# A decoder block on one core: VectorE and ScalarE issue in the order of emission from step 12 to step 172

## The chip, the cores and the metric

The kernel runs on one core of one Trainium2 chip. The metric is the device time of one execution in microseconds (us), the lower the better. The engines are named as the profile names them: PE is TensorE's matmul, PEld its weight load, DVE is VectorE, ACT is ScalarE, POOL is GpSimd, SP is SyncE, which only issues DMAs here. A queue of an engine is told by a q behind its name.

## The reference: what is computed

One decoder layer on 256 tokens of 2048 channels, all in float32. A normalized input goes through one wide projection. Its columns feed two mixers that run beside each other:

- an S5 branch: a state-space scan over the 256 positions (64 groups, 64 complex states each), then GELU, a gated linear unit (GLU) and a projection;
- an attention branch (DSA): a small indexer scores the keys, the 64 best keys of a query stay, then softmax attention on 8 heads, and a projection.

```python
(u, z_ssm, c_q, k, v, z_attn, k_idx, w_idx, gate_ssm, gate_attn) = jnp.split(proj, pts, axis=-1)
y_ssm = s5_branch(u, ...) * jax.nn.silu(z_ssm)
y_attn = dsa_branch(q, k, v, q_idx, k_idx, w_idx) * jax.nn.silu(z_attn)
merged = jax.nn.sigmoid(gate_ssm) * (y_ssm @ w_ssm_out) + jax.nn.sigmoid(gate_attn) * (y_attn @ w_attn_out)
x = x + merged @ w_o
x = x + jax.nn.sigmoid(rms_norm(x, g_ple) @ w_ple_gate) * rms_norm(p @ w_ple, g_ple_post)
return rms_norm(x, g_final)
```

## The kernel before, in words

**Weights in units.** All weights come from HBM in 254 units of up to 128 x 1024 values (tile `raw`, five buffers, 512 KB each, issued by SP on L99). Each unit is split in two parts for the matmul: ACT rounds it to `hi` (`unit_hi`, L261), DVE subtracts it to get the rest, `lo` (`unit_lo`, L273). `hi` and `lo` have four buffers each. PE multiplies each unit in three passes (weights hi, weights lo, and the low part of the input).

**Steps.** One step works on one unit. Step `s` emits, in this order: what the unit needs; the matmuls of unit `s`; `unit_hi(s + 3)` on ACT; the evacuations that are due (`run_deferred`: DVE or ACT reads the PSUM tile of a block that ended a step earlier); `unit_lo(s + 2)` on DVE; the DMA of unit `s + 7` on SP; and then `pump(BUDGET)`. So `lo` is emitted two steps before PE needs it. The units in order: 0 to 15 the S5 input, 16 to 31 its SiLU gate, 32 to 63 one merge gate, 64 to 79 the attention's SiLU gate, 80 to 103 three quarters of the other merge gate, 104 to 131 the query, key, value and indexer projections, 132 to 147 the GLU, 148 to 155 the rest of that gate, 156 to 171 the S5 branch's projection, from 172 on the attention's projection and all that follows. A unit of the gates has 12 matmuls of 512 columns, one of most other projections 24 of 256 columns.

**Threads.** Work that is no weight unit runs in Python generators, which `pump` advances a little in each step: each piece that a generator emits has a cost (`yield 1.15`), `pump` gives out 1.3 a step (at most 3.0 saved up), and `yield ("lag", n)` puts a generator to sleep for n steps. Such threads are the tables of the S5 branch (`s5_tables`, L834 and below), its scan (`s5_gen` with `cmadd`, L950 to L957: 76 DVE operations for each half of the states, two halves), its output (`s5_out`), and the attention (`attn_gen`: scores, the top-k by `max` and `match_replace`, softmax, output of 8 heads). Where a unit needs the end of a thread, the rest of it is emitted at once (`drain`): that is so before step 104, 132 and 172, the last for the attention.

**Order on an engine.** The program is not issued as emitted. A scheduler walks through it on a model of the engines and gives each engine a fixed sequence: of the instructions that its model finds ready, the one emitted first goes first; one that is not ready in the model is passed by later ones. On the chip each engine then follows its sequence, and semaphores hold an instruction until its inputs are there. So DVE's sequence may hold pieces of a thread ahead of a `lo` that was emitted many steps earlier.

The loop that emits the steps is the end of the function below (L1225 and on).

Of the kernel before, what the change touches and what calls it, by code (L numbers as in the profile page):

```python
# [29 lines left out]
NC = 4  # L30
CW = 512
OFF = 16
NWARM = 30
BUDGET = 1.3
TRLAG = 2
# [9 lines left out]
def block_kernel(ctx: ExitStack, tc: tile.TileContext, A: dict, out: bass.AP):  # L45
# [18 lines left out]
    def slot(tag, shape, dt=F32):  # L64
        return cp.tile(shape, dt, tag=tag, name=nm(tag))

    def const(s, shape, dt=F32):
        return cp.tile(shape, dt, tag=s, name=s)
# [19 lines left out]
    def issue_unit(between=None):  # L88
        n = dma_next[0]
        if n >= len(units):  # L90
            return
        c, h, cols = units[n][:3]
        kind, idx = chunks[c]
        r = wp.tile([P, 1024], F32, tag="raw", name=nm("raw"), bufs=5)
        src = (A["wts"][idx] if kind == "w" else A["wvk"][idx])[:, h * cols:(h + 1) * cols]
        q = 2 if between else 1
        for i in range(q):
            s = slice(i * cols // q, (i + 1) * cols // q)
            nc.sync.dma_start(r[:, s], src[:, s])  # L99
            if between and i == 0:  # L100
                between()
        raws[n] = r
        dma_next[0] += 1
# [36 lines left out]
    def mm(o, l, r, start=True, stop=True, **kw):  # L140
        PE.matmul(o, l, r, start=start, stop=stop, **kw)  # L141
# [51 lines left out]
    def run_deferred(flush=False):  # L193
        while True:
            due = [d for d in deferred if flush or d[0] <= step[0]]
            if not due:
                return
            for d in due:
                deferred.remove(d)
            for d in due:  # L200
                d[1]()
# [26 lines left out]
    def pump(budget):  # L228
        credit[0] = min(credit[0] + budget, 3.0)
        while credit[0] > 0:  # L230
            ready = [t for t in threads if t[1] <= step[0]]
            if not ready:
                return
            credit[0] -= advance(ready[0])

    def drain(t):
        while not t[2]:
            advance(t)
# [13 lines left out]
    def unit_hi(u):  # L252
        if u >= len(units):
            return
        cols = units[u][2]
        hi = unit_tile("hi", u)
        src = raws[u][:, :cols]
        q = 2 if u < 3 else 1
        for i in range(q):
            o = slice(i * cols // q, (i + 1) * cols // q)  # L260
            S.copy(hi[:, o], src[:, o])  # L261
        his[u] = hi

    def unit_lo(u):
        if u >= len(units):
            return
        cols = units[u][2]
        lo = unit_tile("lo", u)
        src = raws.pop(u)
        q = 2 if u < 3 else 1  # L270
        for i in range(q):
            o = slice(i * cols // q, (i + 1) * cols // q)
            TT(lo[:, o], src[:, o], his[u][:, o].bitcast(F32), ALU.subtract)  # L273
        los[u] = lo
# [94 lines left out]
    def big_slot(tag, off=0):  # L369
        t = slot(tag, [P, KT * T + OFF], F32R)  # L370
        return t[:, off:off + KT * T].rearrange("p (k t) -> p k t", t=T)
# [254 lines left out]
    def ev_o(nb):  # L626
# [9 lines left out]
        def f(h, ps):  # L636
            if nb == 0 and h == 0:
                R["x2"] = slot("S1", [P, 2, D])
                R["x2h"] = big_slot("XH", OFF)
                R["x2l"] = big_slot("XL", OFF)  # L640
                R["sq2"] = const("sq2", [P, 2, NC])
# [373 lines left out]
    def attn_gen():  # L1015
# [63 lines left out]
        yield ("lag", 1)  # L1079
        ya = big_slot("S7", OFF).rearrange("p (c h) t -> p c h t", c=2)  # L1080
        R["ya"] = ya
# [128 lines left out]
    S.activation(first, mhalf, AF.Copy)  # L1210
    for i in range(NWARM):
        mm(wps[:, :T], warm[:, :P], warm)
# [9 lines left out]
    for i in range(2):  # L1222
        issue_unit()
    NU = len(units)
    for s in range(NU):  # L1225
        step[0] = s
        fn, need = units[s][3:]
        for n in need or ():
            if callable(n):
                n()  # L1230
            else:
                run_deferred()
                drain(R[n])
        fn(his.pop(s), los.pop(s))
        unit_hi(s + 3)
        run_deferred()
        unit_lo(s + 2)
        issue_unit()
        pump(BUDGET)
# [120 lines left out]
```

## Time and profile before

| | us |
|---|---|
| median of three runs | 788.1 |
| the three runs | 788.07, 788.1, 790.91 |
| the profiled execution, its own time | 790.16 |
| its span, from the first to the last instruction | 788.3 |
| PE busy | 766.6 (97%) |
| PEld busy | 668.2 (85%) |
| DVE busy | 576.5 (73%) |
| ACT busy | 392.1 (50%) |
| granted TensorE clock, mean | 0.997 |

The profiled execution is 2.06 us above the median and near the slowest of the three. Matmuls overlap: one of 512 columns shows as 0.39 us busy, while the next starts 0.23 us after it. So a row of PE that follows a wait costs the wait and also the overlap that is lost. The profile puts a wait down to the line whose result came last.

### The profile page before, as it was taken

What the parts mean: (1) busy time and instruction counts of PE and PEld (TensorE: products, weight loads), DVE (VectorE), ACT (ScalarE), POOL (GpSimd) and SP (SyncE); (2) the same over time, 40 slices, a digit from 0 to 9 for tenths busy, and PEclk for the clock granted to TensorE, in tenths of its full rate; (3) what the DMA queues carried; (4) which work ended last, traced back from release to release, by engine and by line L of the source; (5) the groups of instructions that cost most, each with busy time, mean ns of one, the idle gap of its engine ahead of it and who ended that gap; (6) DMA issues with size and microseconds to landing.
All of it is one profiled execution on the core that took longest, in us unless ns stands there. A gap on an engine that the chain in (4) does not pass through costs nothing.

```text
span 788.3 us, 12920 instructions
## 1 busy us (share of the span) xinstructions
PE 766.6 (97%) x5080; PEld 668.2 (85%) x5080; DVE 576.5 (73%) x902; ACT 392.1 (50%) x539; POOL 8.5 (1%) x18
## 2 busy tenths in 40 slices
PE   8999999999999899999999999999999999999995
PEld 6999987786998778899998987887888888888885
DVE  5999953999999964463768988665777855556753
ACT  7544456443433564453645474544446454455642
POOL 0000000000000000000000000000000000000000
PEclk9999999999999999999999999999999999999998
DMA  8768765355665376653664646775875765555622
GB/s 317 274 216 233 239 210 186 111 184 190 220 199 178 125 256 219 216 170 110 226 199 156 207 147 223 248 244 174 287 221 191 261 228 191 184 180 197 213 88 107
DMA packets 52637, 158.08 MB, mean 201 GB/s; under 512 B 5984, under 2 KB 12128, under 8 KB 52192
## 3 DMA queue, kind: packets, MB, share of 16 engines
q1 hardware_dynamic: 47392, 150.15, 57.9%
q10 hardware_dynamic: 5184, 7.10, 2.5%
q8 instruction: 40, 0.66, 0.4%
q14 instruction: 21, 0.17, 0.1%
HBM read 147.79 MB, written 8.39 MB: 198 GB/s over the span
## 4 chain that ended last, share of the span: by engine, by line
PE 47%; issue 1%; DMA 1%; DVE 1%; ACT 0%; POOLq 0%; POOL 0%; DVEq 0%
PE main L141 43%; PE aux L141 3%; PE aux L149 1%; DMA zld<-za_d 1%; DVE t L1086 0%; ACT S L669 0%; DVE S L667 0%; DVE S L668 0%; ACT S L664 0%; DVE S L671 0%; POOLq L1355 0%; POOL r3v L719 0%; DVE S L728 0%; DVEq L1355 0%; DVE S L726 0%
## 5 line engine op out<-in xcount | busy, mean ns | idle before, releaser
L273 DVE TENSOR_TENSOR lo<-raw,hi 128x1024 fp32r<-128x1024 f32 (+2 forms) x255 | 305.2, 1199 | 150.9 <-ACT hi L261 150.8
L261 ACT CAST hi<-raw 128x1024 fp32r<-128x1024 f32 (+2 forms) x255 | 261.6, 1033 | 285.4 <-PE main L141 240.0
L141 PE MATMUL main<-hi,S 128*128 128x512 f32 x512 | 162.6, 393 | 0.0
L141 PE MATMUL main<-lo,XH 128*128 128x512 f32 (+2 forms) x408 | 155.9, 382 | 5.5 <-DVE lo L273 5.5
L141 PE MATMUL main<-hi,XH 128*128 128x512 f32 (+2 forms) x408 | 157.0, 385 | 0.0
L141 PE MATMUL main<-hi,XL 128*128 128x512 f32 (+2 forms) x408 | 155.8, 382 | 0.0
L141 PE MATMUL main<-XH,lo 128*128 128x256 f32 x448 | 124.5, 278 | 1.6 <-DVE lo L273 1.5
L141 PE MATMUL main<-XH,hi 128*128 128x256 f32 x448 | 124.6, 278 | 0.0
L141 PE MATMUL main<-XL,hi 128*128 128x256 f32 x448 | 123.9, 276 | 0.0
L141 PEld LDWEIGHTS main<-hi,S 128*128 128x128 f32 x512 | 96.1, 188 | 19.3
L141 PE MATMUL main<-lo,S 128*128 128x512 f32 x256 | 99.9, 390 | 0.0
L141 PEld LDWEIGHTS main<-lo,XH 128*128 128x128 f32 x408 | 76.8, 188 | 22.2 <-DVE lo L273 8.2
L141 PEld LDWEIGHTS main<-hi,XH 128*128 128x128 f32 x408 | 76.7, 188 | 15.7 <-ACT t L555 0.5
L141 PEld LDWEIGHTS main<-hi,XL 128*128 128x128 f32 x408 | 76.7, 188 | 14.2
L141 PEld LDWEIGHTS main<-XH,lo 128*128 128x128 f32 x448 | 84.1, 188 | 2.8 <-DVE lo L273 2.8
L141 PEld LDWEIGHTS main<-XH,hi 128*128 128x128 f32 x448 | 84.2, 188 | 0.2
L141 PEld LDWEIGHTS main<-XL,hi 128*128 128x128 f32 x448 | 84.2, 188 | 0.1
L141 PE MATMUL main<-S,hi 128*128 128x256 f32 x384 | 67.1, 279 | 0.1
L141 PEld LDWEIGHTS main<-S,hi 128*128 128x128 f32 x384 | 58.1, 188 | 1.7 <-issue 0.7
L141 PEld LDWEIGHTS main<-lo,S 128*128 128x128 f32 x256 | 48.1, 188 | 9.4
L141 PE MATMUL main<-S,lo 128*128 128x256 f32 x192 | 53.1, 277 | 0.0
L141 PEld LDWEIGHTS main<-S,lo 128*128 128x128 f32 x192 | 36.1, 188 | 0.0
(222 smaller groups left out, 677.5 us busy)
## 6 DMA issues: line engine op xcount, KB each, us to landing
raw<-in_wts_dram SPq DMA_DIRECT2D x247, 512.0 KB, 4.3
raw<-in_wvk_dram SPq DMA_DIRECT2D x8, 336.0 KB, 2.9
gs_d<-big ACTq DMA_DIRECT2D x8, 256.0 KB, 3.2
ga_d<-big ACTq DMA_DIRECT2D x8, 256.0 KB, 5.0
big<-gs_d SPq DMA_DIRECT2D x8, 256.0 KB, 4.6
big<-ga_d SPq DMA_DIRECT2D x8, 256.0 KB, 4.4
S<-in_grow_dram SPq DMA_DIRECT2D x2, 1024.0 KB, 7.3
big<-in_xtok_dram SPq DMA_DIRECT2D x8, 256.0 KB, 3.6
```

Of the source, the lines that this page charges most:

```text
L141: PE.matmul(o, l, r, start=start, stop=stop, **kw)
L149: PE.matmul(o, i, idn, is_transpose=True)
L261: S.copy(hi[:, o], src[:, o])
L273: TT(lo[:, o], src[:, o], his[u][:, o].bitcast(F32), ALU.subtract)
```

## The change

From the start of step 12 to the start of step 172 every instruction that is emitted for DVE and for ACT is put into a region in which each of the two engines keeps the order of emission: each instruction there must be issued after the one emitted before it on the same engine. It adds no instruction, removes none, and changes no tile, buffer or DMA. PE, POOL and SP keep the scheduler's order throughout, and so do DVE and ACT before step 12 and from step 172 on. The drain of the attention before step 172 lies behind the region's end, since the region is closed before the unit's needs are looked at; the drains before steps 104 and 132 lie inside it. DMAs that ACT issues (the gates written to HBM, L443 and L451) are in ACT's order too.

```diff
+FIXED = (12, 172)
...
     NU = len(units)
+    order = None
     for s in range(NU):
         step[0] = s
+        if s == FIXED[0]:
+            order = ExitStack()
+            order.enter_context(tc.manual_schedule(engines={mybir.EngineType.DVE, mybir.EngineType.Activation}))
+        if s == FIXED[1]:
+            order.close()
         fn, need = units[s][3:]
```

## Rows read from the trace of the kernel before

**Rows 1.** The page: busy time of the engines, and DVE in 40 slices.
```profile
PE 766.6 (97%) x5080; PEld 668.2 (85%) x5080; DVE 576.5 (73%) x902; ACT 392.1 (50%) x539; POOL 8.5 (1%) x18
...
DVE  5999953999999964463768988665777855556753
```

**Rows 2.** Waits of PE and PEld, 45 to 541 us: total, times, longest.
```profile
PE main L141 <- DVE lo L273: 6.9, 8, 2.3
PE aux L149 <- ACT S L887: 0.6, 1, 0.6
PE aux L141 <- ACT S L887: 0.4, 1, 0.4
...
PEld main L141 <- DVE lo L273: 11.0, 13, 2.7
```

**Rows 3.** Windows: length, busy of PE, PEld, DVE, ACT, POOL, PEclk, DMA.
```profile
45.00:103.00 58.00, 57.00 (x615) 56.37 (x614) 54.91 (x106) 27.91 (x36) 0.00 (x0) 1.00 0.71 215
...
136.00:210.00 74.00, 72.37 (x369) 57.70 (x366) 72.81 (x101) 33.76 (x40) 0.00 (x0) 1.00 0.51 170
210.00:245.00 35.00, 33.49 (x287) 32.70 (x286) 34.62 (x59) 13.51 (x16) 0.00 (x0) 1.00 0.64 207
245.00:284.00 39.00, 35.00 (x360) 29.18 (x360) 38.72 (x56) 20.70 (x26) 0.00 (x0) 1.00 0.48 155
284.00:360.00 76.00, 76.00 (x460) 67.44 (x459) 37.95 (x40) 36.71 (x43) 0.00 (x0) 1.00 0.66 214
...
411.00:482.00 71.00, 70.97 (x521) 63.43 (x521) 58.98 (x117) 41.30 (x65) 1.84 (x3) 1.00 0.54 174
```

**Rows 4.** PE's timeline around the longest wait: start, duration, what, [idle before].
```profile
266.56 0.40 PE L141 MATMUL main<-hi,XL 128*128 128x512 f32 x1
266.79 0.39 PE L141 MATMUL main<-hi,XH 128*128 128x512 f32 x1
269.45 0.49 PE L141 MATMUL main<-lo,XH 128*128 128x512 f32 x1 [2.27 <-DVE lo L273]
269.78 0.40 PE L141 MATMUL main<-hi,XL 128*128 128x512 f32 x1
```

**Rows 5.** DVE's timeline at the scan's first operation and around that wait.
```profile
137.55 1.22 DVE L951 TENSOR_TENSOR S<-S,pre 128x1024 f32<-128x1024 f32 x1
...
265.97 1.19 DVE L953 TENSOR_TENSOR S<-S,psi 128x992 f32<-128x992 f32 x1
267.07 1.19 DVE L955 TENSOR_TENSOR S<-S,S 128x992 f32<-128x992 f32 x1
268.17 1.22 DVE L273 TENSOR_TENSOR lo<-raw,hi 128x1024 fp32r<-128x1024 f32 x1
269.31 1.19 DVE L957 TENSOR_TENSOR S<-S,S 128x992 f32<-128x992 f32 x1
270.41 0.42 DVE L438 TENSOR_TENSOR t<-main,row 128x256 f32<-128x256 f32 x1
270.74 1.22 DVE L273 TENSOR_TENSOR lo<-raw,hi 128x1024 fp32r<-128x1024 f32 x1
...
276.65 1.19 DVE L957 TENSOR_TENSOR S<-S,S 128x992 f32<-128x992 f32 x1
```

**Rows 6.** ACT: waits for evacuations, 45 to 541 us, and one of them.
```profile
ACT big L442 <- DVE t L438: 48.2, 14, 4.6
...
78.86 0.42 ACT L442 ACTIVATE big<-t 128x256 f32<-128x256 f32 x1 [3.12 <-DVE t L438]
...
79.73 2.01 ACT L261 CAST hi<-raw 128x1024 fp32r<-128x1024 f32 x2 [0.45 <-ACT big L442]
```

**Rows 7.** The first softmax: DVE, then ACT, then PE (chain of waits).
```profile
462.21 0.20 DVE L1075 RECIPROCAL sums<-sums 128x8 f32<-128x8 f32 x1 [3.30 <-ACT S L1073]
463.24 1.22 DVE L273 TENSOR_TENSOR lo<-raw,hi 128x1024 fp32r<-128x1024 f32 x1
...
464.71 0.40 ACT L567 CAST S<-t 128x256 fp32r<-128x256 f32 x1
...
468.54 5.71 PE main L141 x24
```

**Rows 8.** The tail of the attention, in the chain of waits.
```profile
537.42 5.19 DMA zld<-za_d
```

## The prediction, made before the result was known

> **What bounds the kernel now.** I read the page first: PE is busy for 97% of the span and DVE for 73%, but DVE's slices stand at nine tenths in three stretches [rows 1]. So PE is the bound on the whole, and the question is what makes it wait, and where. The waits of PE between 45 and 541 us, which is about steps 12 to 172, name one line above all: L273, the `lo` half of a weight unit, made by DVE [rows 2]. PE stood idle for it 8 times, 6.9 us in all; its weight loads waited 13 times, 11.0 us. The windows show where [rows 3]: between 136 and 284 us PE misses 1.63 + 1.51 + 4.00 = 7.1 us, and in the same windows DVE is busy 72.81 + 34.62 + 38.72 = 146.2 of 148 us. Just behind, between 284 and 360 us, PE misses nothing and DVE is busy for only half the time (37.95 of 76 us). DVE is full in one stretch and half empty in the next, and it is late with `lo` in the full one.
>
> What fills it is the scan. It starts at 137.55 us, and its last operation starts at 276.65 us [rows 5]; counting units, PE is in step 41 at the start and in step 84 at the end. The code emits it far more slowly: a half has 24 operations of cost 1.15, 24 of 0.56 and 28 of 0.2, in all 46.6, and at 1.3 a step this takes 36 steps; two halves from step 41 on end at step 113. So DVE's sequence holds operations of the scan up to 29 steps ahead of their place. The longest wait shows what it does: PE, in step 82, needs `lo` of unit 82, which was emitted in step 80. DVE first runs two scan operations at 265.97 and 267.07 us, then this `lo` at 268.17 us [rows 5], and PE's first matmul with it starts at 269.45 us, 2.27 us idle [rows 4].
>
> **The change part by part.** No instruction comes or goes, so DVE's and ACT's busy times stay; only the waits move.
>
> *The `lo` waits.* In the order of emission `lo(s + 2)` stands in step s, ahead of all that step s pumps and behind only what steps up to s emitted. It is late only if DVE itself has fallen behind by more than two steps, less one evacuation and one `lo`: 2 x 2.72 - 0.34 - 1.14 = 4.0 us (a step of 24 matmuls of 256 columns or 12 of 512 is 2.72 to 2.75 us: 12 x 0.23 by rows 4; `lo` and evacuation from start to start, 269.31 - 268.17 and 270.74 - 270.41 [rows 5]). Does it fall behind? A step with the scan holds `lo` 1.14, the scan's 1.3 of budget (an operation of cost 1.15 takes 1.10 from start to start [rows 5]: 1.25), and every second step an evacuation, 0.17 a step: 2.6 us against 2.72. In the steps of the query projection (104 to 113) two operations more come every second step, about 2.9 us a step, so DVE falls 1.5 to 2 us behind there, under the 4.0. In the attention's steps (411 to 482 us) DVE is busy 58.98 of 71 us [rows 3]; the steps of the top-k hold up to 4.5 us, the next ones less, and by my sum over them it is up to 2.5 us behind, again under 4.0. So all of the waits for `lo` go. What they are worth: the idle time, 6.9 us, and the overlap lost at each. At the longest, 2.66 us lie between two starts where 0.23 is usual, so 2.43 are lost for 2.27 idle, and the next start comes after 0.33 instead of 0.23 [rows 4]: 0.26 us beyond the idle time, at each of 13 waits 3.4 us. Sum 10.3 us; the 11.0 us of the weight loads say nearly the same. Bounds: 6.9 and 11.0.
>
> *ACT's order.* The PSUM of the S5 tables was freed late by ACT's copies on L887: PE idle 0.6 + 0.4 us, with two losses of overlap about 1.3 us [rows 2]. ACT was late because its sequence held the SiLU of an evacuation ahead of two `hi`s: it waited 3.12 us for DVE's `t`, and `hi` came after it [rows 6]. There are 14 such waits, 48.2 us. In the order of emission `hi(s + 3)` goes first, and the SiLU stands a step behind its `t`. I take the 1.3 us as gained (bounds 0 and 1.3).
>
> *New waits.* In order, whatever stands behind a waiting instruction waits as well. The worst place is the softmax: DVE waits 3.30 us for ACT's exponentials, and now nothing may pass it. By the rows of before [rows 7] ACT's CAST behind them ends at 465.1 us; the DVE half of it, two evacuation operations and then `lo` of unit 150 follow in order: 465.1 + 3 x 0.34 + 1.2 = 467.3 us, while PE begins unit 150 at 468.54 us and needs `lo` from its second matmul on, at 468.77: 1.4 us to spare. Then come the reciprocal, eight scalings of 0.26 us and `lo` of 151, at 470.9 us against 468.54 + 2.85 + 0.23 = 471.6: 0.7 us to spare. So this costs nothing by the sum, and at the most two softmaxes of 3.3 us, 6.6 us. The scan's end: its last operation is emitted in step 113 and PE's matmuls on it in step 115; with DVE 2 us behind it ends about 4.2 us after step 113 begins, and PE comes to them 8.2 us after that (three steps): 4 us to spare, where before there were 80. I take 1.5 us for all new waits, near the lower end (bounds 0 and 6.6).
>
> *DMA and tail.* SP's order is its own; each `raw` buffer is freed by a `lo`, which now comes earlier, not later. From step 172 on nothing is changed: the wait for the gate's load of 5.19 us [rows 8] stays, give or take 1.5 us.
>
> The sum: -10.3 - 1.3 + 1.5 = -10.1 us on the profiled execution of 790.16 us (span 788.3), so 780.1 us there. That execution is 2.06 us above the median of the runs, which would go from 788.1 to **778.0 us**.
>
> **The rivals.** *(a) Half is given back in the attention.* If ACT's exponentials start 3 us later than before, both margins at the softmax (1.4 and 0.7 us) are gone, and each of two softmaxes costs PE 2 to 3 us: 778 + 5 = 783 us. For it: the margins are thin. Against: DVE's largest reduction can come earlier too, since no later `lo` passes it.
>
> *(b) No change.* If DVE stays as full between 136 and 284 us as it is (146 of 148 us), whatever the order, some `lo` is late: 788 us. It would also be so if the ordering bound only neighbours that already stand in this order. Against: the full stretch is followed by a half-empty one, and the scan's own pace by its costs spreads it over 72 steps instead of 43.
>
> *(c) Slower.* ACT's SiLU waits for DVE's `t`, the next `hi` waits behind the SiLU, the next `lo` for this `hi`, and the next `t` waits behind this `lo`: in a strict order this is a loop. It decides from the point where DVE is more than 3.35 us behind (a step of 2.72 plus ACT's 1.05 for the `hi` ahead of the SiLU, less 0.42 for `t`), in the SiLU steps 16 to 31 and 64 to 79. What then reaches PE is not made up for, since DVE needs 2.6 of each 2.72 us. Of the 48.2 us of such waits, 14 us must reach PE to make the kernel slower by 3.9 us than before; with a third of each (1.1 us, 14 times: 16 us) it comes to 778 + 16 = 794 us. For it: those waits are there in the trace [rows 6]. Against: DVE's load in these steps leaves it at most 1.4 us behind. The Trainium skill speaks for this one: "Perfetto Trace Analysis", section "Tensor Engine Instruction (MATMUL, LD_WEIGHTS)", says that the queues of ACT and DVE are strictly first in, first out, so one waiting instruction holds up all behind it. Rows 6 agree as far as they go: two CASTs ran only after the waiting SiLU. By that rule alone every wait in the new order is dead time; the trace can't show how much of it reaches PE.
>
> **How the numbers follow.** The forecast has a chance of 0.70, and its own range is 775.5 (all 11.0 + 1.3 us gained and no new wait) to 781. Rival (a) has 0.14, (b) 0.08, (c) 0.08. A range to 785.5 us takes in the forecast and (a) and leaves out (b), (c) and a little at the lower end, less than 2 in 10. About 0.5%, 3.9 us, is what a measurement of this kernel can tell from no change. Faster by more than that: the forecast and most of (a), 0.82; within it: (b) and the rest of (a), 0.10; slower: (c), 0.08.
>
> **What would show it.** Right: the waits of PE for L273 between 45 and 541 us are gone or under 1 us; the scan's last operation comes at about 355 us instead of 277; DVE's nines between 136 and 284 us turn to eights, and the half-empty stretch behind fills up; ACT's waits on L442 shrink. The step on new waits is wrong if PE waits for `lo` near the softmaxes or for the scan around 360 us. The whole is wrong if PE still waits 5 us or more for `lo`, or if `hi` takes its place.

## The result and the profile after

The changed kernel takes 779.58 us (median of 4 runs, 779.12 to 780.34); the kernel before, run beside it, 789.0 us (4 runs, 788.07 to 790.91). The ratio is 0.9884, with an interval of 0.987 to 0.9898: about 9.4 us faster. The forecast was 778.0, as a ratio 780.06 / 790.16 = 0.9872. The profiled execution took 779.12 us where 780.1 was forecast (span 777.3, so 11.0 us less than before).

The page of the changed kernel, to be held against [rows 1]:

```profile
PE 766.3 (99%) x5080; PEld 672.2 (86%) x5080; DVE 577.2 (74%) x902; ACT 392.8 (51%) x539; POOL 9.3 (1%) x18
...
DVE  5989883888896898894768978757676755556753
```

The engines did the same work: every busy time is within 1 us of what it was, but PEld's, which shows 4.0 us more. DVE's nines in slices 8 to 14 have become mostly eights, and the sixes and fours in the four slices behind them have become eights and nines. All the waits of PE between 45 and 541 us, and then the one row of its weight loads for `main`, the tile of the weight units, that names another engine, against [rows 2]; the line numbers after are one higher than before:

```profile
PE main L142 <- ACT t L556: 0.3, 1, 0.3
...
PEld main L142 <- ACT t L556: 0.7, 1, 0.7
```

No row names `lo` (L274 now) any more, neither for PE nor for its weight loads, where 6.9 and 11.0 us stood. The windows, with the columns of [rows 3]:

```profile
136.00:210.00 74.00, 74.00 (x395) 61.20 (x394) 63.19 (x92) 35.09 (x41) 0.00 (x0) 1.00 0.61 199
210.00:245.00 35.00, 35.00 (x396) 34.23 (x395) 31.16 (x32) 15.99 (x20) 0.00 (x0) 1.00 0.64 206
245.00:284.00 39.00, 39.00 (x276) 32.85 (x266) 31.57 (x37) 23.59 (x29) 0.00 (x0) 1.00 0.57 190
284.00:360.00 76.00, 76.00 (x648) 68.18 (x647) 58.60 (x94) 31.65 (x38) 0.00 (x0) 1.00 0.50 164
```

PE now misses nothing between 136 and 284 us. DVE is busy there for 63.19 + 31.16 + 31.57 = 125.9 of 148 us instead of 146.2, and for 58.60 instead of 37.95 us in the 76 us behind: some 20 us of the scan have moved there. PE's timeline at unit 82, where before it stood idle for 2.27 us [rows 4], runs through:

```profile
258.83 0.39 PE L142 MATMUL main<-hi,XL 128*128 128x512 f32 x1
259.05 0.39 PE L142 MATMUL main<-hi,XH 128*128 128x512 f32 x1
259.28 0.39 PE L142 MATMUL main<-lo,XH 128*128 128x512 f32 x1
```

DVE's timeline at the scan's end (answers to [rows 5]). The scan's last operation starts at 346.43 us; step 113, which emits it, starts on PE at 344.9 us:

```profile
345.29 1.22 DVE L274 TENSOR_TENSOR lo<-raw,hi 128x1024 fp32r<-128x1024 f32 x1
346.43 1.19 DVE L958 TENSOR_TENSOR S<-S,S 128x992 f32<-128x992 f32 x1
```

Of the 48.2 us that ACT waited for `t` before its SiLU [rows 6], none is left in that stretch.

**Where the 11 us arose.** The two traces are compared at points that are the same place of the program, counted in PE's matmuls with weight units. Near 45 us the changed kernel is 0.23 us behind in this execution: the same matmul stands in the kernel before at

```profile
45.00 0.28 PE L141 MATMUL main<-XH,hi 128*128 128x256 f32 x1
```

and after at

```profile
45.23 0.28 PE L142 MATMUL main<-XH,hi 128*128 128x256 f32 x1
```

Then PE's first matmul of step 104, where it switches from 512 to 256 columns, in the kernel before:

```profile
331.62 0.28 PE L141 MATMUL main<-XH,hi 128*128 128x256 f32 x1
```

and after:

```profile
319.48 0.28 PE L142 MATMUL main<-XH,hi 128*128 128x256 f32 x1
```

So this stretch takes 286.62 us before and 274.25 us after: 12.37 us are won, against 11.6 forecast for `lo` and L887 together, and the lead at step 104 is 331.62 - 319.48 = 12.14 us. Then pieces of the chain of waits (start, duration, what), before:

```profile
387.92 12.52 PE main L141 x108
400.65 13.62 PE main L141 x120
...
427.52 19.25 PE main L141 x168
...
478.50 19.34 PE main L141 x84
...
772.33 9.29 issue
```

and after:

```profile
377.08 12.53 PE main L142 x108
389.83 14.14 PE main L142 x120
...
417.13 19.98 PE main L142 x168
...
469.08 19.33 PE main L142 x84
...
761.64 9.29 issue
```

The lead is 387.92 - 377.08 = 10.84 us, then 10.82, 10.39, 9.42 and 10.69. So 2.7 us are lost again between steps 104 and 153, and 1.3 us are won around step 172. At most of the places where they are lost PE waits for nothing: the same 120 matmuls take 14.14 us instead of 13.62, and the same 168 take 19.98 instead of 19.25. The last section comes back to this. The profile's span differs by another 0.3 us behind these rows.

### The profile page after: what moved, and what is told of

It reads as the page before. It is cut to its first block, busy times and chain, and to the rows that moved or that the text cites. A ratio compares the mean times of both kernels' runs of the same rounds, so it can differ in the third digit from the quotient of the medians.

```text
span 777.3 us, 12902 instructions
## 1 busy us (share of the span) xinstructions
PE 766.3 (99%) x5080; PEld 672.2 (86%) x5080; DVE 577.2 (74%) x902; ACT 392.8 (51%) x539; POOL 9.3 (1%) x18
## 4 chain that ended last, share of the span: by engine, by line
PE 48%; issue 1%; ACT 1%; DVE 0%; POOLq 0%; POOL 0%; DVEq 0%
PE main L142 43%; PE aux L142 4%; PE aux L150 1%; ACT S L1074 0%; ACT L556 0%; ACT hi L262 0%; ACT S L670 0%; DVE S L668 0%; DVE S L669 0%; ACT S L665 0%; DVE S L672 0%; POOLq L1362 0%; POOL r3v L720 0%; DVE S L729 0%; DVE S L727 0%
## 5 line engine op out<-in xcount | busy, mean ns | idle before, releaser
L274 DVE TENSOR_TENSOR lo<-raw,hi 128x1024 fp32r<-128x1024 f32 (+2 forms) x255 | 304.1, 1197 | 93.1 <-ACT hi L262 92.3
```

## The experiments

Each was compared with runs of the kernel before on the same chip: the medians of those were 789.25 us for the first four below and 788.61 us for the next four. All diffs but the eighth are against the changed kernel.

**1. The order for DVE alone.**

```diff
-            order.enter_context(tc.manual_schedule(engines={mybir.EngineType.DVE, mybir.EngineType.Activation}))
+            order.enter_context(tc.manual_schedule(engines={mybir.EngineType.DVE}))
```

> The region orders DVE alone; ACT keeps the scheduler's order. Theory (the gain is DVE's: lo no longer stands behind the scan): the waits of PE for lo between 45 and 535 us are gone, about 10 us of the 11 us of the change, time near 780 us; PE's waits for ACT's copies of the S5 tables may stay (1.3 us). Rival (ACT's order carries it, since late hi make late lo): 785 us or more, waits for lo of 4 us or more.

Measured: 780.1 us, ratio 0.9887 (0.9872 to 0.9902): the whole gain. PE's waits between 45 and 541 us, all of them:

```profile
PE aux L150 <- DVE t L1087: 0.3, 1, 0.3
PE main L142 <- ACT t L556: 0.3, 1, 0.3
```

The wait for ACT's copies (L888 now) is gone as well, with ACT in the scheduler's order. ACT still waits for `t` before a SiLU, 10.5 us in 5 waits, but less than the 48.2: DVE's order alone brings `t` earlier.

**2. The order for ACT alone.**

```diff
-            order.enter_context(tc.manual_schedule(engines={mybir.EngineType.DVE, mybir.EngineType.Activation}))
+            order.enter_context(tc.manual_schedule(engines={mybir.EngineType.Activation}))
```

> The region orders ACT alone; DVE keeps the scheduler's order. Theory: the scan still runs ahead, PE still waits 6 to 7 us for lo, only the wait for the S5 tables' copies goes: 787 to 788 us. Rival (ACT's order carries it): 782 us or less. Rival (strict order as a loop: a waiting SiLU holds hi): slower than before, 792 us.

Measured: 790.56 us, ratio 1.0013 (0.9999 to 1.0027). PE's waits between 45 and 541 us, all of them:

```profile
PE main L142 <- DVE lo L274: 7.2, 7, 3.2
```

ACT's order changes nothing that can be measured in the time, and the waits for `lo` are as large as before. The wait for ACT's copies (L888) is gone here too. And with ACT in strict order and DVE as full as before (73.21 of 74 us in the window from 136 us), the kernel is not measurably slower; the whole loop of rival (c) needs DVE in order as well, which is the changed kernel.

**3. Only where the scan is emitted: steps 36 to 116.**

```diff
-FIXED = (12, 172)
+FIXED = (36, 116)
```

> The region, both engines, reaches from step 36 to 116 only: the steps in which the scan is emitted. Theory: nearly all of the gain on lo, 10 us, but not the 1.3 us of the tables' copies before step 31: about 780 us. Rival (the attention's or the tables' steps carry a good part): 784 us or more.

Measured: 780.19 us, ratio 0.9884 (0.9867 to 0.99). Again the whole gain; no row of PE's waits names `lo`.

**4. Only ahead of it: steps 12 to 36.**

```diff
-FIXED = (12, 172)
+FIXED = (12, 36)
```

> The region, both engines, reaches from step 12 to 36 only: the steps of the S5 tables. Theory: the 1.3 us of PE's waits for the tables' copies go, the scan runs ahead as before and PE waits 6.5 us or more for lo: 787 to 788 us. Rival (what runs ahead early decides all that follows): 783 us or less.

Measured: 788.35 us, ratio 0.999 (0.998 to 1.0001). `lo` is still waited for:

```profile
PE main L142 <- DVE lo L274: 4.7, 6, 2.2
```

**5. Only the attention: steps 116 to 172**, the test of rival (a).

```diff
-FIXED = (12, 172)
+FIXED = (116, 172)
```

> The region, both engines, reaches from step 116 to 172 only: the last projections, the GLU and the attention. Theory: nothing is gained or lost there, 788 to 789 us, PE's waits for lo stay at 6.5 to 7 us and lie before 284 us. Rival (a) of the prediction (strict order costs PE 2 to 3 us at each softmax): 791 us or more. Rival (these steps carry a part of the gain): 786 us or less.

Measured: 788.73 us, ratio 0.9996 (0.9982 to 1.0009). The order costs the softmaxes nothing that can be measured. Its rows of waits hold 7.0 us for `lo`, as before, and at the softmax the same 0.3 us (ACT's `t`, L556) as in the changed kernel.

**6. One step more: the drain ahead of step 172 inside the region.**

```diff
-FIXED = (12, 172)
+FIXED = (12, 173)
```

> As after, but the region is closed a step later, at 173, so that the drain of the attention (the last heads, emitted one after the other at once) lies inside it. Theory: an order of emission is good only where it is spread over the steps; here copy, product, rounding and rest of one head stand ahead of the next head's, a chain of about 3 us a head on ACT and DVE, so PE waits: 3 to 6 us slower than after, 783 to 786 us. Rival (PE has enough other work): 779 to 780 us.

Measured: 785.54 us, ratio 0.996 (0.9946 to 0.9974): some 6 us of the gain are lost, most of them at one place. All of PE's waits between 515 and 560 us:

```profile
PE main L142 <- DVE lo L274: 2.6, 1, 2.6
PE aux L150 <- DVE t L1087: 1.2, 1, 1.2
PE aux L142 <- ACT S L1103: 1.2, 1, 1.2
```

and DVE's timeline there, in which L1087 and L1093 are the drain's operations:

```profile
530.79 0.42 DVE L1087 TENSOR_TENSOR t<-aux,zld 128x256 f32<-128x256 f32 x1 [2.31 <-DMA zld<-za_d]
...
540.03 0.42 DVE L1087 TENSOR_TENSOR t<-aux,zld 128x256 f32<-128x256 f32 x1 [0.99 <-PE aux L142]
540.92 0.43 DVE L1093 TENSOR_TENSOR S<-t,S 128x256 fp32r<-128x256 f32 x1 [0.47 <-ACT S L1090]
541.26 4.63 DVE L274 TENSOR_TENSOR lo<-raw,hi 128x1024 fp32r<-128x1024 f32 x4
```

The drain is emitted in one piece ahead of the unit, so in the order of emission four `lo`s stand behind all its operations, and each of these waits in turn for a load, for PE or for ACT. DVE is idle most of this time and may not use it. This is what rival (c) feared, at another place: a chain of short operations that wait, put ahead of `lo`. The Trainium skill says it of the queues ("Perfetto Trace Analysis", section "Tensor Engine Instruction (MATMUL, LD_WEIGHTS)": ACT and DVE are strict FIFO); the `lo` that comes only at 541.26 us agrees with it.

**7. `lo` one step ahead instead of two**, and one weight unit less loaded ahead, to measure how far DVE falls behind.

```diff
-    unit_lo(1)
...
-    for i in range(2):
+    for i in range(1):
         issue_unit()
...
-        unit_lo(s + 2)
+        unit_lo(s + 1)
```

> As after, but lo is emitted one step before its use instead of two (and a unit's DMA six steps before instead of seven, since lo frees its buffer a step later). What DVE may be behind falls from 4.0 us to about 1.3. Theory (DVE falls up to 2 us behind in the query projection and 2.5 in the attention): PE waits for lo 3 to 8 us in these two stretches, 783 to 788 us. Rival (DVE is hardly ever behind): 779 to 781 us. Rival (every step is tight): 795 us or more.

Measured: 784.61 us, ratio 0.9942 (0.9927 to 0.9957), some 5 us slower than the changed kernel; the profiled execution, 782.88 us, is the fastest of six. The waits of its weight loads for `lo`, the longest of them, in step 140, and PE between 411 and 482 us, in the attention's steps:

```profile
PEld main L142 <- DVE lo L274: 4.7, 10, 1.0
...
426.36 0.19 PEld L142 LDWEIGHTS main<-S,lo 128*128 128x128 f32 x1 [0.97 <-DVE lo L274]
...
411.00:482.00 71.00, 69.72 (x468) 60.83 (x467) 61.25 (x128) 37.76 (x62) 2.85 (x3) 1.00 0.50 167
```

So the second step of lead is used: without it `lo` comes up to 1.0 us late. Of the ten waits, five (2.1 of the 4.7 us) lie in the attention's steps 140 to 149, and PE misses 1.28 us in that window, where it misses 0.25 in the changed kernel. One of 0.35 us comes just behind the query projection, in step 115. The other four lie elsewhere, from 54 to 528 us; none had been expected there.

**8. The scan alone.** No region: the kernel before, in which each of the scan's operations (four lines, L951 to L957) must only be issued after the `lo` emitted last ahead of it.

```diff
-            TT(lo[:, o], src[:, o], his[u][:, o].bitcast(F32), ALU.subtract)
+            R["lo_ins"] = TT(lo[:, o], src[:, o], his[u][:, o].bitcast(F32), ALU.subtract).ins
...
-                TT(w0, src, cr, ALU.mult)
+                with tc.issue_after(R["lo_ins"]):
+                    TT(w0, src, cr, ALU.mult)
...
```

> The kernel before, with no region. Only the 152 operations of the scan get one order each: after the lo that was emitted last before them. All else on DVE and ACT stays the scheduler's. Theory (the scan that runs ahead of lo is the one cause): PE's waits for lo between 45 and 535 us fall from 6.9 us to under 1 us, time 780 to 781 us. Rival (the order of evacuations, tables or attention against lo has a good part in it): 784 us or more.

Measured: 780.48 us, ratio 0.9895 (0.9879 to 0.991). With nothing but this one relation the gain is there, within the interval. All of PE's waits between 45 and 541 us:

```profile
PE aux L149 <- DVE t L1090: 0.9, 1, 0.9
PE aux L141 <- ACT S L887: 0.2, 1, 0.2
```

**9. Both kernels once more**, for their profiles alone (no edit). The changed kernel:

> The changed kernel once more, for its profile alone. In the first profile the matmuls of 256 columns between 318 and 353 us and between 390 and 438 us start every 117.8 ns, elsewhere every 113.3 ns, at a granted clock of 1.00 in both, and PE waits for nothing there: some 2.5 us that the sum of the prediction did not hold. If the new order of DVE and ACT sets the slower pace, the same stretches are slow again, and the total is within 1 us of 779.6. If it is a state of the chip that comes and goes, the slow stretches lie elsewhere or are missing, and the total moves by up to 3 us.

and the kernel before:

> The kernel before once more, for its profile alone. If the pace is set by the order of the work, its matmuls in steps 104 to 115 and 129 to 143 start every 113.3 ns again, as in its first profile. If the pace comes and goes by itself, one of these stretches may now stand at 117.8 ns, with 1.3 us more for each.

Measured: 779.69 and 790.2 us. The second profile of the kernel before has PE's waits of the same kind, in other sizes than [rows 2]:

```profile
PE main L141 <- DVE lo L273: 5.5, 6, 2.9
PE aux L141 <- ACT S L887: 0.2, 1, 0.2
```

The idle time is 5.7 us here instead of 7.9, and yet the stretch from near 45 us to step 104 takes 286.4 us, as in the first profile (286.6). One reason is the clock: when PE had stood idle for 2.9 us in step 82, the granted clock was 0.56 between 267 and 270 us and 0.58 in the next 5 us, mostly the lower of its two levels (1.2 instead of 2.4 GHz). These 5 us, in the first profile of the kernel before and in the second:

```profile
270.00:275.00 5.00, 5.00 (x23) 3.94 (x21) 5.00 (x6) 4.11 (x6) 0.00 (x0) 1.00 0.72 229
...
270.00:275.00 5.00, 5.00 (x14) 3.87 (x14) 5.00 (x6) 4.97 (x9) 0.00 (x0) 0.58 0.53 181
```

That is 9 matmuls fewer, some 2 us at 0.23 us each, and no wait shows them. It does not always come: behind the same wait the clock fell in experiments 2 and 4 too (0.75 and 0.76 in this window), but not in the first profile and not in experiment 5 (1.00). What the pace of the matmuls did is told in the last section.

None of these versions beats the changed kernel: those without the slack or with the drain in order are slower, those with the whole gain lie within its interval. PE stands idle for 0.3 us between 45 and 541 us of its first profile and for 1.2 us of its second, so another order has hardly any idle time left to win in that stretch.

## Why the prediction was right

**The cause.** Experiments 3 to 5 and experiment 8 carry it, from two sides. With the order in steps 36 to 116 alone, the gain is whole and outside of them it is nothing; with the scan alone held behind `lo`, it is whole too. So it is the scan ahead of `lo`, as the prediction said, and neither the tables nor the attention. That DVE is not too full in the region, which was the point against rival (b), the windows of after show.

**The size.** The term for `lo` (10.3) and that for L887 (1.3) make 11.6 us; 12.37 were won from 45 us to step 104, of which, matmul by matmul, about 1.2 lie at the two waits for L887 and the rest, about 11.1, at `lo`: the upper of my two bounds (11.0) was the nearer one. The idle time that went is 6.9 + 0.6 + 0.4 = 7.9 us. The other 4.5 us are 0.30 us at each of 13 + 2 waits, if all of it is put down to lost overlap there; I had 0.26 from a single one. Those who read only the idle time of PE would have forecast a third less. The second profile of the kernel before holds one more price of a wait that the sum did not have, the granted clock behind it (experiment 9). The term on L887 was sized from one execution: that second profile shows 0.2 us of it instead of 1.0, and 5.5 us for `lo`. Its attribution to ACT's order is not shown: the wait is gone with DVE's order alone (experiment 1) and with ACT's alone (experiment 2), and a wait that differs so much between two executions can't be put down to either. The lower end of the range, 775.5, doesn't follow from its own terms, which give 788.1 - 12.3 = 775.8.

**The new waits.** 1.5 us were set down for them. As waits they are 0.3 us: at the softmax DVE stands idle longer for ACT (5.03 us, for a rounding that ACT does behind the exponentials, where it was 3.30 us for the exponentials themselves), yet both margins for `lo` held. The one wait that came is at a place that I had not looked at, ACT's own evacuation behind the exponentials. The chain of waits after:

```profile
451.04 1.48 ACT S L1074 x6
...
454.76 0.39 ACT t L556
...
455.20 3.27 PE main L142 x13
```

PE waits there for what ACT does on L556, 0.26 us. Rival (a) fell by its condition: the exponentials do not come later. ACT begins the first softmax's, before and after, at

```profile
456.83 1.28 ACT L1073 ACT_TABLE_LOAD   x1
...
447.17 1.28 ACT L1074 ACT_TABLE_LOAD   x1
```

which is 9.66 us apart, just the lead that PE's own matmuls have there; PE is in the same matmul of step 146 both times. Of the 2.7 us lost again by step 153 the other 2.4 went to a slower pace of the matmuls (last section), which no term held. That they don't show in the total is luck: the first terms were 0.8 us too small, the new waits 1.2 us too large, and the tail gave 1.3 us.

**The slack.** DVE was to be at most 2.5 us behind, with 4.0 us allowed. Experiment 7 takes a step of 2.72 us from the allowance, which leaves 1.3, and `lo` is late by up to 1.0 us: a lag of about 2.3 us, in step 140, in the attention, for which 2.5 was worked out. Behind the query projection it is 0.35 us late, a lag of about 1.6 us, for which 1.5 to 2 was worked out. Size and place were right, as far as one trace shows; the waits at four other places were not in the sum.

**The scan's end** was forecast for about 355 us and came at 346.43. The step was right, 113; I had read its time off the trace of before, where PE starts step 113 at 356.1 us, and had not taken off the 11 us that the change wins ahead of it.

**The tail** was to stay, give or take 1.5 us, and gave 1.3. In the stretch from 515 to 560 us PE waits for nothing in this execution (45.00 of 45 us busy, before 43.71), but it misses 0.9 us there in its second profile: it varies from one execution to the next, so I do not count the gain to the change.

**Rival (c)** fell by the result itself: both engines are in order, and ACT's waits for `t` before its SiLU are gone. Experiment 6 shows what it would take: a drain in one piece.

**The median.** The kernel before came out at 789.0 us beside the changed one instead of 788.1; that is 0.9 of the 1.6 us by which 778.0 was missed.

## What to carry to other kernels

An engine that is nine tenths busy in one stretch and half empty in the next can be a matter of order: look which long, patient work runs ahead of its place, and what short work on the critical path stands behind it. Holding that one kind of work behind the urgent one gave the whole gain here; an order for whole engines gave no more, and did harm where a piece of dependent work is emitted in one go. Price a wait of PE by the distance between matmul starts, not by its idle time, look at the granted clock behind it, and look at two executions before a small wait gets a term of its own.

## What the runs showed that I had not expected

PE's matmuls of 256 columns go at one of two paces in whole stretches, at a granted clock of 1.00 in both. Ten of them apart, in the timeline of the changed kernel, a few steps after step 104 begins:

```profile
330.44 0.28 PE L142 MATMUL main<-XH,hi 128*128 128x256 f32 x1
...
331.61 0.28 PE L142 MATMUL main<-XL,hi 128*128 128x256 f32 x1
```

and in the kernel before, in step 104:

```profile
332.54 0.28 PE L141 MATMUL main<-XH,lo 128*128 128x256 f32 x1
...
333.68 0.28 PE L141 MATMUL main<-XH,hi 128*128 128x256 f32 x1
```

1.17 against 1.14 us; over longer rows it is 117.8 ns a matmul against 113.4, and PE waits for nothing in either. A step of 24 takes 0.1 us longer. The slow pace stands between 318 and 354 us and again in most of 390 to 438 us, in both profiles of the changed kernel and in those of experiments 1, 3, 6 and 8, which have no wait for `lo` there either. In neither profile of the kernel before is it there in steps 104 to 115. But the order doesn't set it alone: the second profile of the kernel before has it between 207 and 234 us (in the attention's SiLU gate, whose units have 24 matmuls of 256 columns and not the 12 of 512 told above for gates) and around 390 us, where its first has not. The chain of waits of that second profile, to be held against the 12.52 us shown above for the same 108 matmuls:

```profile
387.63 12.99 PE main L141 x108
```

So both expectations on it hold in part: the stretches come back with the changed kernel, and the pace also comes and goes by itself. Two more traces speak against the missing waits and against the order as its cause. Experiment 5 waits for `lo` as the kernel before does (7.0 us) and has the scheduler's order up to step 116, yet the slow pace is there from step 104 on. Experiment 7 has the order and hardly a wait for `lo` ahead of step 104, yet its steps 104 to 115 go at the fast pace. The same 120 matmuls as above, in experiment 5 and then in experiment 7:

```profile
400.74 14.14 PE main L142 x120
...
390.00 13.62 PE main L142 x120
```

What makes the difference stays open. It takes up to 2.5 us here, more than all the new waits.
